# Rows for the gather written once, the accumulator filled by a DRAM copy, and weight splits moved between engines

## The chip, the cores and the metric

One core of a Trainium2 chip runs the kernel. The metric is the device time of one execution in microseconds (us); the median of several executions counts. The engines are named as in the profile: PE is TensorE (PEld its weight loads), DVE is VectorE, ACT is ScalarE, POOL is GpSimd, SP is SyncE, which here only issues DMAs.

## The reference, cut to what matters

One encoder layer over L = 528 tokens (16 meta tokens and 512 real ones) of width 1024. Two attention branches give `oa` and `ob`; these are merged, projected and added to the residual `h`. Then each of 16 experts picks the 66 tokens with the highest affinity to it.

```python
merged = sigmoid(ga) * (oa @ w_branch_a) + sigmoid(gb) * (ob @ w_branch_b)
h = h + merged @ w_out
u = rms_norm(h, g_ffn)
aff = softmax(u @ w_router)                       # (528, 16)
top_aff, top_idx = top_k(aff.T, 66)               # per expert
xs = u[top_idx]                                   # (16, 66, 1024)
y = (silu(xs @ w_gate) * (xs @ w_up)) @ w_down * top_aff
h = h.at[top_idx].add(y)                          # rows are added up
return rms_norm(h, g_final)[16:]
```

## The kernel before

Everything is float32. A product is made of three passes of TensorE: each operand is split into a high half (rounded to the matmul's type) and a low half (the rest), and high x high, low x high and high x low are added up. The helper `hi_lo` (line 440) does one split: ScalarE casts the high half, then VectorE, or the engine that is handed in, subtracts it from the source.

**Order of work.** Instructions for ScalarE, VectorE and GpSimd are not issued where they stand: `Pace` (line 126) keeps them in a list, prices them, follows a model of the engines' clocks and issues the one that can start, a lower `prio` number first. TensorE's instructions and DMAs go out where they stand in the program. Every engine then runs its own list in order, and so do the DMA queues of SP and GpSimd.

**Projections.** `project` (line 500) computes one block of 128 output features for all 528 tokens, in two parts of 256 and 272 columns, 24 matmuls each. It is a generator that yields after 6, 12, 18 and 24 matmuls of a part, so that its caller can put other products between. The weights of the block after it are split inside it by `split_weights` (line 484), in two halves of 128x512; `spare_engine` (line 444) hands the subtraction to GpSimd unless its clock in the model is far ahead. Blocks go by numbers `j`; `jof["yb", 0]` is the first block of w_branch_b, and the eight blocks of w_out come after the eight of w_branch_b.

**w_out and the router** (lines 1298 to 1356). For block d of w_out the evacuation adds the residual into `h2T` (the new `h`, features on the partitions), splits it into `hh` and `hl`, and squares it for the norm. Router products of block d (`sums`) and the column sums of the squares (`ones_sum`) are put into `routed` and taken out of it while block d+1 runs, one after each of the first yields. In the last block (d = 7), ahead of it, the first of the experts' weight pieces is split (`split_piece(0)`, line 1347), the subtraction on GpSimd.

**Routing** (lines 1357 to 1477). `put_rows(t)` turns 88 tokens of `h2T` into rows (8 transposes, two copies by ScalarE) and stores them twice over SP's queue: 1024 wide into `acc`, the accumulator in DRAM to which experts add, and, in `send_rows` (line 1388), 1028 wide into `urow`, from which experts gather, once GpSimd has put the token's norm factor behind its row. There are six groups of 88; the last is stored in two parts, since the meta tokens stand last in the work and first in DRAM. Meanwhile VectorE computes the softmax `lg` and nine rounds of top-k (lines 1448 to 1456), and from both halves of the tokens the list `idxu`. Between, pieces 1 and 2 of the first expert's weights are split (lines 1433 and 1434), on GpSimd again.

**Experts** (lines 1481 to 1701). `gather(e)` fetches 66 rows of `urow` by an indirect DMA of GpSimd; `spread_x(e)` turns them back and applies `g_ffn`; the norm factor comes in as a scale after the first products. The weights are 48 matrices of 2 MB (`mats`, in order of use: gate 0, up 0, gate 1, down 0, up 1, gate 2, down 1, up 2, ...), each used in four pieces of 128x1024, which are split a few pieces ahead. Matrices 1 and on go through a ring of eight buffers (line 1210): matrix n uses buffer (n - 1) mod 8. `load_mat` (line 1221) loads matrices up to 7 over SP's queue and later ones over GpSimd's, matrix 7 in two halves, the second (`load_rest`) over GpSimd's queue behind the first gathers. `scatter(e)` adds the expert's rows to `acc` by an accumulating indirect DMA of GpSimd.

Of the kernel before, what the change touches and what calls it, by code (L numbers as in the profile page):

```python
# [10 lines left out]
F32 = mybir.dt.float32  # L11
F32R = mybir.dt.float32r
# [8 lines left out]
P = 128  # L21
D = 1024
S = 512
M = 16
L = S + M
HL = L // 2
LX = L + 2 * M
DX = D + 4
HALF = [slice(0, 256), slice(256, L)]
NC = D // P  # L30
# [39 lines left out]
def keys(ap):  # L70

    kind = ap.name.split("_")[0]
    step = ap.ap[0][0]
    width = {"kbuf": L, "m1": L, "h2T": L, "xin": D, "pair": L, "obf": L, "hrow": D, "junk": D, "big": D, "first": D, "raw": D,
             "hid": FF // 2, "hhl": 2 * CAP, "xg": 4 * CAP}.get(kind, step)
    rows = {"zp": 32, "kbuf": 64, "qh": 64, "ql": 64, "kbh1": 64, "kbl1": 64}.get(kind, P) if K["kr"] else P
    if width == step and rows == P:
        return {ap.name}
    low, first = divmod(ap.offset, step)
    last = first + sum((n - 1) * s for s, n in ap.ap[1:])  # L80
    high = low + ap.ap[0][1] - 1
    return {f"{ap.name}/{j}/{i}" for i in range(first // width, last // width + 1)
            for j in range(low // rows, high // rows + 1)}
# [209 lines left out]
def block_kernel(ctx: ExitStack, tc: tile.TileContext, x, meta_tokens, g_mix, w_cols,  # L293
# [3 lines left out]
    pace = Pace()  # L297
    Pace.LAT, Pace.AHEAD = K["lat"], K["ahead"]
    nc = Engines(pace, tc.nc)
# [18 lines left out]
    wk = pool(ctx, "wk")  # L318
    psum = pool(ctx, "psum", space=PSUM)
    acc = dram.tile([L, D], F32, name="acc")  # L320
    urow = dram.tile([L, DX], F32, name="urow")
# [78 lines left out]
    def until(*tiles):  # L400

        for _ in range(400):
            if all(pace.when(a) <= pace.now() for a in tiles):
                break
            pace.t["tensor"] = pace.now() + 100.0
            pace.pump()
# [33 lines left out]
    def hi_lo(hi, lo, src, eng=None):  # L440
        nc.scalar.copy(hi, src)
        (eng or nc.vector).tensor_sub(lo, src, hi.bitcast(F32))

    def spare_engine():
        return nc.gpsimd if pace.t.get("gpsimd", 0.0) < pace.now() + K["spare"] else nc.vector
# [25 lines left out]
    loaded, split = {}, {}  # L471
# [12 lines left out]
    def split_weights(j, upto=2):  # L484
        if j >= len(stream):
            return
        load_weights(j)
        if j not in split:
            split[j] = (wk.tile([P, NC, P], F32R, tag="wh", bufs=2, name="wh"),
                        wk.tile([P, NC, P], F32R, tag="wl", bufs=2, name="wl"), [0])  # L490
        wh, wl, done = split[j]
        while done[0] < upto:
            b = slice(4 * done[0], 4 * done[0] + 4)
            with rank(pace, "split"):
                hi_lo(wh[:, b], wl[:, b], loaded[j][:, b], spare_engine())
            done[0] += 1
            if done[0] == 2:
                Task(load_later(j + 3), Need([wl]))
# [42 lines left out]
    jof = {}  # L541
# [17 lines left out]
    xin = [keep.tile([P, 2, D], F32, tag=t, name="xin") for t in ("o_l", "o_h")]  # L559
# [81 lines left out]
    m1 = keep.tile([P, NC, L], F32, tag="m1", name="m1")  # L641
# [329 lines left out]
    kbuf = keep.tile([P, 2, 4, L], F32R, tag="obf", name="kbuf")  # L971
# [107 lines left out]
    obf = keep.tile([P, NH, L], F32, tag="obf", name="obf")  # L1079
# [59 lines left out]
    for h in range(NH):  # L1139
        todo = dict(q=lambda: proj_q(h + 1), k=lambda: proj_k(1), v=lambda: proj_v(1),  # L1140
                    g=lambda: gate_a(h + 1), y=lambda: branch_a(h))
# [15 lines left out]
    pc = pool(ctx, "pc")  # L1157
    mg_h = pc.tile([P, NC, L], F32R, tag="mg_h", name="mg_h")
    mg_l = pc.tile([P, NC, L], F32R, tag="mg_l", name="mg_l")
# [18 lines left out]
    h2T = keep.tile([P, NC, L], F32, tag="obf", name="h2T")  # L1178
# [33 lines left out]
    raws = {}  # L1212
# [3 lines left out]
    def load_rest():  # L1216
        for raw, src in rest:
            nc.gpsimd.dma_start(raw, src)
        rest.clear()

    def load_mat(n, parts=1):
        if n >= len(mats) or n in raws:
            return
        src, kc, f = mats[n]
        src = src.rearrange("(c p) f -> p c f", p=P)
        if n == 0:
            raws[n] = [pc.tile([P, 2, f], F32, tag=("xa", "xb")[i % 2], bufs=2, name="first") for i in range(4)]
            for i, raw in enumerate(raws[n]):
                nc.sync.dma_start(raw, src[:, 2 * i:2 * i + 2])
                raws[n][i] = raw.rearrange("p c f -> p (c f)")  # L1230
            return
        pool_, tag = ring[(n - 1) % len(ring)]
        raw = pool_.tile([P, kc, f], F32, tag=tag, name="raw")
        eng = nc.gpsimd if n > 7 else nc.sync
        cut = kc // parts
        eng.dma_start(raw[:, :cut], src[:, :cut])
        if parts > 1:
            rest.append((raw[:, cut:], src[:, cut:]))
        raw = raw.rearrange("p c f -> p (c f)")
        raws[n] = [raw[:, 1024 * i:1024 * (i + 1)] for i in range(4)]  # L1240

    places = []
    for _ in range(2):
        pair = pc.tile([P, 2, L], F32, tag="ys", bufs=2, name="pair")
# [24 lines left out]
    pieces = {}  # L1269
    whole = {len(mats) - 4: None, len(mats) - 1: None}  # L1270
    nextraw = [9]
    wh, wl, xa, xb = (wk, "wh"), (wk, "wl"), (pc, "xa"), (pc, "xb")
    spots = [(xb, wl), (wh, wl), (xa, xb), (xa, wh)]

    def split_piece(k):
        n, i = divmod(k, 4)
        if n >= len(mats) or k in pieces:
            return
        load_mat(n)
        src = raws[n][i]  # L1280
        if n in whole:
            if i == 0:
                whole[n] = [keep.tile([P, 4, 1024], F32R, tag=tag, name="big") for tag in ("u_h", "u_l")]
            hi, lo = whole[n][0][:, i], whole[n][1][:, i]
        else:
            tags = spots[i if k else 1]
            hi, lo = [pool_.tile([P, 1024], F32R, tag=tag, bufs=2, name=name)
                      for (pool_, tag), name in zip(tags, ("eh", "el"))]
        prio, pace.prio = pace.prio, 2 if n < len(mats) - 2 else K["sp"]
        hi_lo(hi, lo, src, nc.gpsimd if k < 3 or n in whole and i > 1 else None)  # L1290
        pace.prio = prio
        pieces[k] = hi, lo
        if i == 3 and k > LOOK:
            while nextraw[0] <= min(n + len(ring) - (n - 1) // K["skip"], len(mats) - 3):
                load_mat(nextraw[0])
                nextraw[0] += 1
# [46 lines left out]

    load_mat(0)
    for d in range(NC):
        if d == NC - 1:
            split_piece(0)
        g = project(jof["wo", d], mg_h, mg_l, route(d))
        todo = len(routed)
        for n, _ in enumerate(g):  # L1350
            if n < todo:
                routed.pop(0)()
        if d in K["ld"]:
            load_mat(3 + K["ld"].index(d))
# [4 lines left out]
    TQ, NT, HT = 88, 6, 3  # L1359
# [9 lines left out]
    rowq = []  # L1369

    def put_rows(t):
        row = (pc.tile([TQ, DX], F32, tag="ys", bufs=2, name="row") if t == 3 else
               wk.tile([TQ, DX], F32, tag="wraw", bufs=3, name="row"))
        for b in range(2):
            pt = ptr()
            for c in range(4):
                tr(pt[:TQ, c * P:(c + 1) * P], h2T[:, 4 * b + c, t * TQ:(t + 1) * TQ])
            nc.scalar.copy(row[:, 512 * b:512 * b + 512], pt[:TQ, :])
        send(acc, t, row, D)
        rowq.append((t, row))  # L1380

    def send(dst, t, row, w):
        n = TQ if t + 1 < NT else S - t * TQ
        nc.sync.dma_start(dst[M + t * TQ:M + t * TQ + n, :], row[:n, :w])
        if n < TQ:
            nc.sync.dma_start(dst[:M, :], row[n:, :w])

    def send_rows():

        for t, row in rowq:  # L1390
            nc.gpsimd.tensor_copy(row[:, D:], rc[:, t:t + 1].to_broadcast([TQ, DX - D]))
            send(urow, t, row, DX)
        rowq.clear()

    pace.prio = 1
    put_rows(0)
# [15 lines left out]
    rs, rc, sm = cc[:, 1, :NT], cc[:, 1, NT:], cc[:, 3, :NT]  # L1412
# [13 lines left out]
    nc.vector.reciprocal(sm, sm)  # L1426
    nc.vector.tensor_mul(lg, lg, wide(sm))
    pace.prio = 1
    put_rows(1)
    put_rows(2)  # L1430
    pace.prio = 0
    until(lg)
    split_piece(1)
    split_piece(2)
    pf = pz()
    for i in range(HT):
        tr(pf[:2 * NE, i * TQ:(i + 1) * TQ], lg[:, 2 * i:2 * i + 2, :].rearrange("p h e -> p (h e)"))
    pace.prio = 1
    send_rows()
    for t in range(3, NT):  # L1440
        put_rows(t)
        send_rows()
    load_mat(7, parts=2)

    pace.prio = 0
    rounds = (CAP + 7) // 8
# [28 lines left out]
    nc.vector.tensor_tensor(affc, lists[:, 0, 0], vb_, op=OP.max)  # L1475

    until(idxu)
    pace.prio = 1
    xsplit = {}

    def gather(e):
        if e >= NE:
            return
        xs = wk.tile([CAP, DX], F32, tag="wraw", bufs=3, name="xs")
        nc.gpsimd.indirect_dma_start(out=xs, out_offset=None, in_=urow,
                                     in_offset=bass.IndirectOffsetOnAxis(ap=idxu[:, e:e + 1], axis=0))
        xsplit[e] = xs
# [56 lines left out]

    gather(0)
    gather(1)
    gather(2)
    load_rest()
    load_mat(8)
    pace.prio = 0  # L1550
    until(xsplit[0])
# [228 lines left out]
```

## Time and profile before

| | before |
|---|---|
| median of 3 runs | 1058.24 us (1058.0 to 1058.52) |
| the profiled execution itself | 1060.26 us |
| its span, first to last instruction | 1058.5 us |
| TensorE / VectorE / ScalarE / GpSimd busy | 91% / 69% / 60% / 35% |
| mean granted TensorE clock, share of full speed | 0.974 |
| DMA: moved in all | 186.43 MB |

The profile is of one execution. "Busy" counts instructions in execution; matmuls are pipelined, so a busy TensorE need not be at its peak. A row in square brackets names the idle time in front of an instruction and what ended it. All instructions bear line 199 (L199), because one helper issues them all; they are told apart by their tiles, output first ("hl<-h2T,hh"). The blocks of w_out run from about 659 to 719 us, routing to 752 us, the experts to the end.

### The profile page before, as it was taken

The numbers are of one execution on the slowest core, as the hardware profiler recorded it, in microseconds if no ns is written. First come the engines' busy times: TensorE is split into PE (matmuls) and PEld (weight loads), VectorE is DVE, ScalarE is ACT, GpSimd is POOL, SyncE is SP. The second block draws the span as 40 slices with busy tenths as digits, with TensorE's granted clock in tenths as the row PEclk, the third lists the DMA queues.
The fourth block names the chain that finished last, engine by engine and source line by source line (L and its number), as shares of the span: only waits on it lengthen the run. The fifth ranks groups of instructions, "written<-read, shape, count | busy, mean of one in ns | idle before, by whom it ended". The sixth has DMA issues, their size and how long they took to land.

```text
span 1058.5 us, 18096 instructions
## 1 busy us (share of the span) xinstructions
PE 964.3 (91%) x6835; PEld 831.8 (79%) x6835; DVE 726.4 (69%) x1354; ACT 630.2 (60%) x1297; POOL 368.4 (35%) x395
## 2 busy tenths in 40 slices
PE   5799999999999999999999999985599999999984
PEld 4799989999889899999999999873356666666562
DVE  6357777767775666665653345566499999999885
ACT  5366656665655455555554533334388888888773
POOL 3233232333443343443333334432224342424153
PEclk9999999999999999999999999997699999999997
DMA  7544434443222221221212555816799999999964
GB/s 249 168 128 102 134 116 128 132 113 102 68 57 68 71 67 55 71 63 59 71 44 81 160 167 197 326 51 226 244 326 375 337 381 326 377 350 355 343 175 184
DMA packets 59405, 186.43 MB, mean 176 GB/s; under 512 B 6298, under 2 KB 6439, under 8 KB 59318
## 3 DMA queue, kind: packets, MB, share of 16 engines
q1 hardware_dynamic: 32950, 87.96, 26.8%
q0 software_dynamic: 25760, 95.16, 26.2%
q10 hardware_dynamic: 608, 2.16, 0.6%
q8 instruction: 54, 0.88, 0.3%
q14 instruction: 33, 0.27, 0.1%
HBM read 162.07 MB, written 10.76 MB: 163 GB/s over the span
## 4 chain that ended last, share of the span: by engine, by line
PE 61%; DVE 14%; ACT 8%; issue 6%; DMA 5%; POOL 5%; SPq 2%; POOLq 0%; ACTq 0%; DVEq 0%
PE pz L199 36%; PE psc L199 19%; PE ptr L199 5%; DVE sn L199 3%; POOL cols L199 3%; ACT sn L199 2%; SPq L199 2%; DVE cols L199 1%; DVE pb L199 1%; DVE hl L199 1%; DMA raw<-in_w_down_dram 1%; DVE wtl L199 1%; DVE zb L199 1%; DVE ls L199 1%; DMA zp<-zb 1%
## 5 line engine op out<-in xcount | busy, mean ns | idle before, releaser
L199 POOL TENSOR_TENSOR wl<-wraw,wh 128x512 fp32r<-128x512 f32 x137 | 185.3, 1362 | 406.0 <-ACT wh L199 399.6
L199 PE MATMUL pz<-u_h,wh 128*128 128x256 f32 (+1 forms) x832 | 246.2, 296 | 5.7 <-DVE kbuf L199 1.7
L199 PE MATMUL pz<-u_h,wl 128*128 128x256 f32 (+1 forms) x832 | 238.1, 286 | 0.6 <-DVE wl L199 0.6
L199 PE MATMUL pz<-u_l,wh 128*128 128x256 f32 (+1 forms) x832 | 238.0, 286 | 0.5 <-DVE u_l L199 0.5
L199 DVE TENSOR_TENSOR el<-raw,eh 128x1024 fp32r<-128x1024 f32 x180 | 213.9, 1228 | 6.2 <-ACT eh L199 4.9
L199 ACT CAST eh<-raw 128x1024 fp32r<-128x1024 f32 x180 | 182.0, 1049 | 23.8 <-PE pz L199 15.1
L199 PEld LDWEIGHTS pz<-u_h,wh 128*128 128x128 f32 x832 | 158.1, 190 | 9.0 <-DVE kbuf L199 2.3
L199 PEld LDWEIGHTS pz<-u_l,wh 128*128 128x128 f32 x832 | 158.3, 190 | 0.6 <-DVE u_l L199 0.6
L199 PEld LDWEIGHTS pz<-u_h,wl 128*128 128x128 f32 x832 | 157.9, 190 | 0.8 <-DVE wl L199 0.8
L199 PE MATMUL psc<-eh,xh 128*66 128x512 f32 (+1 forms) x272 | 105.1, 386 | 2.7 <-ACT hid L199 2.2
L199 ACT CAST wh<-wraw 128x512 fp32r<-128x512 f32 x152 | 90.9, 616 | 24.0 <-PE pz L199 11.4
L199 PE MATMUL psc<-el,xh 128*66 128x512 f32 (+1 forms) x272 | 104.0, 382 | 0.9 <-DVE el L199 0.9
L199 PE MATMUL psc<-eh,xl 128*66 128x512 f32 (+1 forms) x272 | 104.0, 382 | 0.0
L199 DVE TENSOR_TENSOR wtl<-ptr,wth 128x512 fp32r<-128x512 f32 (+1 forms) x72 | 46.0, 638 | 59.1 <-ACT wth L199 58.8
L199 PE MATMUL pz<-eh,hhl 128*66 128x512 f32 x224 | 70.6, 396 | 0.7 <-DVE hhl L199 0.6
L199 POOL DMA_INDIRECT acc<-ys,idxu x15 | 28.7, 1911 | 119.9 <-ACT ys L199 117.6
L199 ACT ACTIVATE sn<-sn,nm 128x528 f32<-128x528 f32 x64 | 47.1, 736 | 35.2 <-DVE nm L199 34.8
L199 ACT CAST wth<-ptr 128x512 fp32r<-128x512 f32 (+1 forms) x72 | 39.1, 543 | 40.3 <-PE ptr L199 39.9
L199 PEld LDWEIGHTS psc<-eh,xh 128*66 128x66 f32 x272 | 37.5, 138 | 25.4 <-ACT hid L199 3.2
L199 PEld LDWEIGHTS psc<-el,xh 128*66 128x66 f32 x272 | 37.3, 137 | 24.4 <-DVE el L199 1.4
L199 PEld LDWEIGHTS psc<-eh,xl 128*66 128x66 f32 x272 | 37.4, 138 | 21.8 <-issue 0.6
L199 DVE CUSTOM_DVE_ANT_0 sn<-psc,m 128x528 f32<-128x528 f32 x64 | 44.1, 695 | 6.7 <-PE psc L199 6.7
(314 smaller groups left out, 2341.2 us busy)
## 6 DMA issues: line engine op xcount, KB each, us to landing
wraw<-in_w_in_dram SPq DMA_DIRECT2D x76, 512.0 KB
raw<-in_w_gate_dram POOLq DMA_DIRECT2D x13, 2048.0 KB, 14.6
raw<-in_w_down_dram POOLq DMA_DIRECT2D x13, 2048.0 KB, 16.1
raw<-in_w_up_dram POOLq DMA_DIRECT2D x13, 2048.0 KB, 14.9
m<-in_c_bias_dram SPq DMA_DIRECT2D x8, 1056.0 KB
kbuf<-kbuf SPq DMA_DIRECT2D x32, 132.0 KB
raw<-in_w_up_dram SPq DMA_DIRECT2D x2, 2048.0 KB
raw<-in_w_gate_dram SPq DMA_DIRECT2D x2, 2048.0 KB
```

Of the source, the lines that this page charges most:

```text
L199: op.fn(*op.args, **op.kw)
```

## The change

Five things change. (1) From w_branch_b's first block on VectorE subtracts in every weight split. (2) The products in `routed` are taken out after the 12th matmul of the first part and the 6th and 18th of the second, where before it was after the 6th, 12th and 18th of the first part. (3) A row is stored once, 1024 wide, into `urow`; rows 2 to 5 have a tile of their own in a buffer that w_out leaves free (`mg_l`); the norm factors are widened by one GpSimd instruction and stored behind all rows (`send_factors`). (4) `acc` is filled by one DMA from `urow` on GpSimd's queue behind gathers 0 and 1, and matrix 7 is loaded whole on that queue just ahead of it. (5) Pieces 0 to 2 are no longer split on GpSimd in w_out and in routing: the high halves of pieces 0 and 1 are cast behind the rows (`start_piece`), and their low halves and piece 2 follow on VectorE behind the list.

```diff
@@ split_weights @@
-                hi_lo(wh[:, b], wl[:, b], loaded[j][:, b], spare_engine())
+                hi_lo(wh[:, b], wl[:, b], loaded[j][:, b], nc.vector if j >= jof["yb", 0] else spare_engine())
@@ load_mat @@
-        eng = nc.gpsimd if n > 7 else nc.sync
+        eng = nc.gpsimd if n > 6 else nc.sync
@@ new, ahead of split_piece @@
+    def start_piece(k):
+        hi, lo = [wk.tile([P, 1024], F32R, tag=tag, bufs=2, name=name) for tag, name in (("wh", "eh"), ("wl", "el"))]
+        prio, pace.prio = pace.prio, 2
+        nc.scalar.copy(hi, raws[0][k])
+        pace.prio = prio
+        return hi, lo
@@ split_piece @@
-        hi_lo(hi, lo, src, nc.gpsimd if k < 3 or n in whole and i > 1 else None)
+        hi_lo(hi, lo, src, nc.gpsimd if n in whole and i > 1 else None)
@@ blocks of w_out @@
-        if d == NC - 1:
-            split_piece(0)
         g = project(jof["wo", d], mg_h, mg_l, route(d))
         todo = len(routed)
         for n, _ in enumerate(g):
-            if n < todo:
+            if n in (1, 4, 6)[:todo]:
                 routed.pop(0)()
@@ routing @@
     def put_rows(t):
-        row = (pc.tile([TQ, DX], F32, tag="ys", bufs=2, name="row") if t == 3 else
-               wk.tile([TQ, DX], F32, tag="wraw", bufs=3, name="row"))
+        if t == 2:
+            rowq.append(pc.tile([TQ, 4, D], F32, tag="mg_l", name="rowp"))
+        row = (rowq[0][:, t - 2] if t > 1 else pc.tile([TQ, D], F32, tag="ys", bufs=2, name="row") if t else
+               wk.tile([TQ, D], F32, tag="wraw", bufs=3, name="row"))
...
-        send(acc, t, row, D)
-        rowq.append((t, row))
+        send(urow, t, row)
...
-    def send_rows():
-        for t, row in rowq:
-            nc.gpsimd.tensor_copy(row[:, D:], rc[:, t:t + 1].to_broadcast([TQ, DX - D]))
-            send(urow, t, row, DX)
-        rowq.clear()
+    def send_factors():
+        rc4 = pc.tile([TQ, NT, DX - D], F32, name="rc4")
+        nc.gpsimd.tensor_copy(rc4, rc.unsqueeze(2).to_broadcast([TQ, NT, DX - D]))
+        n = NT - 1
+        nc.sync.dma_start(urow[M:M + n * TQ, D:].rearrange("(t p) w -> p t w", p=TQ), rc4[:, :n])
+        send(urow, n, rc4[:, n], slice(D, DX))
...
-    put_rows(1)
-    put_rows(2)
+    for t in range(1, 4):
+        put_rows(t)
     pace.prio = 0
     until(lg)
-    split_piece(1)
-    split_piece(2)
...
-    send_rows()
-    for t in range(3, NT):
+    for t in range(4, NT):
         put_rows(t)
-        send_rows()
-    load_mat(7, parts=2)
+    send_factors()
+    firsts = [start_piece(k) for k in range(2)]
...
     until(idxu)
+    for k, (hi, lo) in enumerate(firsts):
+        nc.vector.tensor_sub(lo, raws[0][k], hi.bitcast(F32))
+        pieces[k] = hi, lo
+    split_piece(2)
...
     gather(0)
     gather(1)
+    load_mat(7)
+    nc.gpsimd.dma_start(acc, urow[:, :D])
     gather(2)
-    load_rest()
     load_mat(8)
```

## Rows read from the trace of the kernel before

**Rows 1.** The page, first part: busy us (share of the span) xinstructions.
```profile
PE 964.3 (91%) x6835; PEld 831.8 (79%) x6835; DVE 726.4 (69%) x1354; ACT 630.2 (60%) x1297; POOL 368.4 (35%) x395
```
**Rows 2.** Waits of PE, 540 to 720 us: us in total, times, longest.
```profile
PE psc L199 <- DVE hl L199: 6.4, 8, 2.0
```
**Rows 3.** Timeline around one w_out block's start: start us, us, instruction [idle before].
```profile
690.95 0.43 DVE L199 TENSOR_TENSOR hl<-h2T,hh 128x256 fp32r<-128x256 f32 x1 [0.47 <-ACT hh L199]
...
693.69 2.74 POOL L199 TENSOR_TENSOR wl<-wraw,wh 128x512 fp32r<-128x512 f32 x2 [4.27 <-ACT wh L199]
...
694.01 1.27 DVE L199 TENSOR_TENSOR hl<-h2T,hh 128x272 fp32r<-128x272 f32 x1 [0.48 <-ACT hh L199]
...
694.40 0.28 PE L199 MATMUL pz<-mg_h,wl 128*128 128x256 f32 x1
...
694.52 0.29 PE L199 MATMUL psc<-hh,wr 128*32 128x272 f32 x1
...
695.34 0.30 PE L199 MATMUL psc<-hl,wr 128*16 128x272 f32 x1 [0.53 <-DVE hl L199]
```
**Rows 4.** Timeline of PE in the last w_out block.
```profile
708.55 0.29 PE L199 MATMUL psc<-hh,wr 128*32 128x272 f32 x1
710.87 0.30 PE L199 MATMUL psc<-hl,wr 128*16 128x272 f32 x1 [2.03 <-DVE hl L199]
...
712.63 0.28 PE L199 MATMUL psc<-qql,ones 128*2 128x256 f32 x1 [0.47 <-DVE qql L199]
```
**Rows 5.** Instructions on tile wl, 600 to 720 us: ns min/median/max, first and last start.
```profile
L199 DVE TENSOR_TENSOR wl<-wraw,wh x2: 692/996/1301, 599.6 to 612.7; 128x512 fp32r<-128x512 f32 x2
```
**Rows 6.** Stretches: length; PE, PEld, DVE, ACT, POOL busy; PEclk, DMA share, GB/s.
```profile
613.00:663.00 50.00, 50.00 (x411) 49.67 (x410) 26.30 (x51) 16.74 (x36) 22.50 (x17) 1.00 0.58 191
663.00:702.00 39.00, 36.17 (x291) 34.25 (x289) 22.70 (x32) 14.72 (x35) 15.67 (x13) 1.00 0.65 241
746.00:786.00 40.00, 33.20 (x152) 19.96 (x153) 28.34 (x34) 26.61 (x32) 12.36 (x15) 0.85 0.86 284
787.00:805.00 18.00, 18.00 (x88) 10.96 (x87) 16.85 (x19) 15.31 (x19) 6.30 (x6) 1.00 1.01 361
```
**Rows 7.** Timeline of ACT, then of DVE, in the routing.
```profile
723.33 1.06 ACT L199 COPY row<-ptr 88x512 f32<-88x512 f32 x2 [0.30 <-PE ptr L199]
724.84 0.28 ACT L199 ACTIVATE lg<-lg 88x96 f32<-88x96 f32 x1 [0.45 <-DVE lg L199]
...
732.75 1.06 ACT L199 COPY row<-ptr 88x512 f32<-88x512 f32 x2 [4.65 <-DMA urow<-row]
...
739.49 0.17 DVE L199 TENSOR_TENSOR idxu<-take,ptr 66x16 uint32<-66x16 f32 x1
```
**Rows 8.** Timeline of SP's DMA issues in the routing.
```profile
721.14 3.56 SPq L199 DMA_DIRECT2D acc<-row  x3
```
**Rows 9.** The chain that ended last, merged: start us, us, what.
```profile
740.68 3.85 DMA urow<-row
...
745.51 6.00 DMA xs<-urow,idxu
...
776.44 0.51 PE ptr L199 x8
...
988.42 9.73 PE psc L199 x42
```
**Rows 10.** Timeline of DVE and POOL around two later gathers.
```profile
825.29 3.48 DVE L199 TENSOR_TENSOR el<-raw,eh 128x1024 fp32r<-128x1024 f32 x3
...
825.51 1.88 POOL L199 DMA_INDIRECT xs<-urow,idxu  x1 [0.21 <-POOL rsx L199]
...
872.39 1.02 POOL L199 DMA_INDIRECT xs<-urow,idxu  x1 [0.21 <-POOL rsx L199]
```
**Rows 11.** Weight loads issued at 763.44 and 958.16 us: KB, us to landing.
```profile
raw<-in_w_down_dram POOLq DMA_DIRECT2D x1, 2048.0 KB, 8.0
...
raw<-in_w_gate_dram POOLq DMA_DIRECT2D x1, 2048.0 KB, 24.3
```

More of the change, by code (lines that the diff above doesn't have):

```diff
@@ L73, in keys @@
     step = ap.ap[0][0]
-    width = {"kbuf": L, "m1": L, "h2T": L, "xin": D, "pair": L, "obf": L, "hrow": D, "junk": D, "big": D, "first": D, "raw": D,
+    width = {"kbuf": L, "rowp": D, "m1": L, "h2T": L, "xin": D, "pair": L, "obf": L, "hrow": D, "junk": D, "big": D, "first": D, "raw": D,
              "hid": FF // 2, "hhl": 2 * CAP, "xg": 4 * CAP}.get(kind, step)
@@ L1285, in split_piece @@
         else:
-            tags = spots[i if k else 1]
+            tags = spots[i]
             hi, lo = [pool_.tile([P, 1024], F32R, tag=tag, bufs=2, name=name)
@@ L1378, in put_rows, with send @@
             nc.scalar.copy(row[:, 512 * b:512 * b + 512], pt[:TQ, :])
-        send(acc, t, row, D)
-        rowq.append((t, row))
-    def send(dst, t, row, w):
+        send(urow, t, row)
+    def send(dst, t, row, cs=slice(0, D)):
         n = TQ if t + 1 < NT else S - t * TQ
-        nc.sync.dma_start(dst[M + t * TQ:M + t * TQ + n, :], row[:n, :w])
+        nc.sync.dma_start(dst[M + t * TQ:M + t * TQ + n, cs], row[:n])
         if n < TQ:
-            nc.sync.dma_start(dst[:M, :], row[n:, :w])
-    def send_rows():
-        for t, row in rowq:
-            nc.gpsimd.tensor_copy(row[:, D:], rc[:, t:t + 1].to_broadcast([TQ, DX - D]))
-            send(urow, t, row, DX)
-        rowq.clear()
+            nc.sync.dma_start(dst[:M, cs], row[n:])
+    def send_factors():
[4 more added lines that the diff above has]
+        send(urow, n, rc4[:, n], slice(D, DX))
     pace.prio = 1
```

## The prediction, written before the change was run

> **What bounds the kernel now.** I read the page first: TensorE is busy for nine tenths of the span [rows 1], so a change pays only where TensorE waits, in the rest. Then the waits of TensorE, the timeline around the longest, the chain of waits through the routing, and last the DMA issues of the expert phase.
>
> In the projection by w_out TensorE waits eight times for hl, VectorE's low half of the residual stream, 6.4 us in all [rows 2]. One block shows the cause [rows 3]: VectorE's subtraction for the first half of the columns takes 0.43 us; that for the second takes 1.27 us, and it runs while GpSimd subtracts the next weights (2.74 us for two). TensorE starts the router product that needs it at 695.34, where its step before (694.40 to 694.52) would put it at 694.64.
>
> Routing is one chain: softmax, top-k, list of rows (idxu), gather, first expert. The list is there at 739.49 + 0.17 = 739.66 [rows 7], but the first gather starts at 745.51, behind the last store into urow, which lands at 744.53 [rows 9]. Those stores are late because a row tile is free only when its second store has landed (ScalarE idles 4.65 us for that [rows 7]) and because SP issues fourteen stores, 1.2 us each in [rows 8].
>
> In the expert loop TensorE does not wait (18.00 us busy of 18), while the DMA engines are full, at 361 GB/s [rows 6]: there the change can only lose.
>
> **The change, part by part.** The sum is made against the profiled execution, 1060.26 us: a span of 1058.5 and 1.76 around it. The median of the runs is 2.02 us lower, 1058.24; I take the gain off that, as nothing ties the difference to a place.
>
> *Weight splits of w_branch_b and w_out from GpSimd to VectorE; router products later.* Each of six blocks (d = 1 to 6) loses 695.34 - 694.64 = 0.70 us: 4.20. In the last block GpSimd also splits the first weight piece, and the losses are 710.87 - 708.55 - 0.12 = 2.20 and, for the column sums, 0.47 [rows 4]. Both halves of the edit take them away: GpSimd no longer subtracts beside VectorE, and the second product, now 12 matmuls into the next block, comes 30 in, some 2 us later. Gain 6.87. The wait behind the last block, with no block to hide it, stays. VectorE pays 32 subtractions of 0.69 us (the shorter of its two, the other ran beside GpSimd) [rows 5]: 1.4 us per block, in two stretches where it was busy 26.3 of 50 and 22.7 of 39 us [rows 6]; the products that need them start a block later. If that cover is gone, a block waits up to 0.69: 16 of them, 11 us. Bounds: 4 and 7.5 gained with the cover, 4 lost without it.
>
> The Trainium skill, "SBUF — State Buffer", section "Who interferes with whom", has a VectorE instruction with two SBUF inputs and a GpSimd one that reads SBUF exclude each other for a whole instruction. The trace agrees: 0.43 against 1.27 us.
>
> *The chain to the gather.* Gone are the second stores with their landing, and two weight pieces' splits in front of row 3's copies. All rows are then turned one behind the other. Row 2 is copied by 723.33 + 1.06; three more at 1.06 and 0.3 us for the gap, and 1 us for Exp and the transposes of the softmax's output between, make 729.5 on the old clock of events. SP needs to 731 to send the last (two stores), and 3.85 of landing [rows 9] make 735. The factors, in stores of 16-byte pieces, have no like in the trace: sent at once, 1.5 us of issue and the same landing, they are there at 736.4; held until the rows have landed, at 740.3. I take the first, since SP sent stores to different rows of one tensor without waiting [rows 8]; the second costs 0.6. So the gather waits for the list. With the 0.98 us between release and start that the chain has (744.53 to 745.51 [rows 9]) it starts at 740.64, a gain of 4.87.
>
> Three things go off. Row 3's first copy (half of 1.06) may stand ahead of the softmax's Exp [rows 7]: 0 to 0.5, taken 0.25. VectorE now computes the low halves of pieces 0 to 2 right behind the list: three took 3.48 us [rows 10], hidden under the gather's 6.00 [rows 9]; but a gather issued while VectorE subtracts took 1.88 us against 1.02 with VectorE idle [rows 10]: 0 to 0.9, taken 0.86. The transfer may be shorter than 6.00 without a weight load beside it: 0 to 1 gained, taken 0. Net 4.87 - 1.11 = 3.76, bounds 2.8 and 6.
>
> By the section just named a subtraction leaves GpSimd's write side free, so what it holds at a gather could only be the read of the list; if that read came first, nothing would be held and the sum would be 0.86 better. Rows 10 show one held.
>
> *The copy within DRAM, and matrix 7 behind the gathers.* GpSimd's queue gets, behind gather 1, the whole of matrix 7 (before, SP loaded half of it ahead of the gathers), the copy of 2.16 MB, then gather 2 and matrix 8, and every later load stands behind these. SP loses seven stores into acc, which lay under the top-k but for their place between the urow stores. No row has a transfer from DRAM to DRAM. Lower bound: a load of nearly its size, with no other load in front, landed in 8.0 us [rows 11]. Upper: its bytes are read and written, so twice that, 16.0. I take 11, nearer the load, since reads and writes can overlap.
>
> Added work is 2.9 us (1.05 MB at 361 GB/s) and 11; the engines were idle 14% of 746 to 786, 5.6 us [rows 6]. So later loads land up to 8.3 us later, and stay so, since DMA is full from 787 on. The tightest load I found is the gate of expert 14: issued at 958.16, landed at 982.5 [rows 11]. Its first product follows 24 of the run of 42 that starts at 988.42 and takes 9.73 [rows 9]: 994.0, less 2.3 us of splitting: 9.2 us of slack. It covers 8.3; up to 11.9 us of copy nothing waits. Gather 2, also behind the copy, is wanted 776.44 - 745.51 = 30.9 us after the start of gather 0 [rows 9], with 6.0 (gather), 5.8 (2.1 MB) and 11 us of transfers before its own: some 8 us of room. Taken: 0; at 16 us the loss is 4.1.
>
> The Trainium skill, "DMA: Bandwidth & Descriptors", section "Specifications", gives some 358 GB/s of HBM per core; as an estimate the copy, 4.32 MB in both directions, would take 12.1 us by it and the sum would be 0.2 us worse. No row here tests it.
>
> Sum: 6.87 + 3.76 - 0 = 10.63, so 1049.6 for the execution that was profiled and 1058.24 - 10.63 = **1047.6 us** for the median.
>
> **The rivals.**
> *Weights late.* The copy takes 12 to 20 us. For it: late loads already land after 24.3 us. Against: DMA had idle time just where the copy goes. 16 us give 1047.6 + 4.1 = 1051.7. Chance 0.17.
> *The gather still waits for urow,* by factors that are held or small pieces that land slowly: 0.6 to 3 us, 1048.2 to 1050.6. For it: the last store bounds the gather today. Against: 3 us of room. Chance 0.11.
> *VectorE becomes the bound* of the two projections, so that the first part loses 4 where it should gain 6.87: 1058.5, no change. For it: one of its two weight splits took about 1.3 us. Against: half its time is free, and a split has a block's lead. Chance 0.04.
> *Slower: the copy blocks the weight stream.* It decides from 11.9 + 10.6 = 22.5 us of copy (96 GB/s): then what every expert's weights come late is more than the gain. At 30 us: 1047.6 + 18.1 = 1065.7. For it: nothing shows how fast DRAM to DRAM goes, and one queue carries it and the weights. Against: 528 rows of 4 KB spread over the engines like the weights. Chance 0.05.
> *More than forecast:* gather not held and shorter, 1044 to 1045.7. Chance 0.08.
>
> **How the numbers follow.** The forecast has 0.55, its own range 1045.7 to 1049.8. To take in a copy of 16 us and a late gather I give 1044.5 to 1052.0; outside lie the two cases at 1058 and beyond, the worse part of the late weights, and a little below. A measurement of this kernel tells 0.2%, 2.1 us, from no change. Faster: forecast, late weights, late gather and more, 0.91. Same: VectorE, 0.04. Slower: 0.05.
>
> **What would show it.** After: no wait of TensorE for hl in the w_out blocks, that behind the last one ending near 711.5; VectorE's hl at 0.43 and its weight splits at 0.69 us. The list near 733.0; the first gather within a microsecond of it, released by VectorE and not by a store; the first expert product near 742.7. The landing time of the copy, and no wait of TensorE for el before the last two experts. I am wrong if a store releases the gather, if weights make TensorE wait, or if the span is not near 1047.9.

## The result, and the profile after

The changed kernel takes 1047.8 us (median of 4 runs, 1047.58 to 1050.28), the kernel before 1058.38 us beside it (1058.0 to 1060.21): a ratio of 0.989, 95% interval 0.9874 to 0.9905. The forecast was 1047.6. A second run of the changed kernel, on another chip, gave 1048.31 us against 1059.26, a ratio of 0.9888 (0.9866 to 0.9911).

The profiled execution took 1047.58 us, its span 1045.8, which is 12.7 less than before. Five starts cut both spans into stretches that can be laid side by side: w_out's first projection matmul, its last, the list, the first gather, the first expert product.

| stretch | before, us | after, us | gain | predicted |
|---|---|---|---|---|
| ahead of w_out | 658.95 | 657.63 | 1.32 | 0 |
| w_out, first to last projection matmul | 57.63 | 50.45 | 7.18 | 6.87 |
| to the list | 22.91 | 23.07 | -0.16 | -0.25 |
| list to first gather | 6.02 | 1.21 | 4.81 | 4.87 |
| first gather to first expert product | 7.77 | 7.46 | 0.31 | -0.86 |
| first expert product to the end | 305.22 | 305.98 | -0.76 | 0 |

The first row can't be told from the spread: over all the profiles of the changed kernel and its variants w_out starts anywhere from 657.19 to 659.56 us. It is 1.32 of the 2.1 us by which the two profiled executions differ more than the two medians do.

**w_out.** TensorE's waits of 540 to 720 us, answering [rows 2]: one for hl is left of eight, the one behind the last block (us in total, times, longest).

```profile
PE psc L199 <- DVE hl L199: 1.2, 1, 1.2
PE pz L199 <- DVE lg L199: 1.2, 1, 1.2
```

The timeline of a block, answering [rows 3]: VectorE's weight split takes 0.69 us and hl 0.44, for 1.27 before; hl is there at 696.85, the product that reads it comes at 698.99 and waits for nothing. The last two lines are TensorE's first and last projection matmul in w_out.

```profile
695.80 0.69 DVE L199 TENSOR_TENSOR wl<-wraw,wh 128x512 fp32r<-128x512 f32 x1
696.41 0.44 DVE L199 TENSOR_TENSOR hl<-h2T,hh 128x272 fp32r<-128x272 f32 x1
...
698.87 0.29 PE L199 MATMUL psc<-hh,wr 128*32 128x272 f32 x1
698.99 0.29 PE L199 MATMUL psc<-hl,wr 128*16 128x272 f32 x1
...
657.63 0.29 PE L199 MATMUL pz<-mg_h,wh 128*128 128x256 f32 x1
...
708.08 0.29 PE L199 MATMUL pz<-mg_h,wl 128*128 128x272 f32 x1
```

**Routing.** The timeline of ScalarE, SP, VectorE and GpSimd, answering [rows 7 and 8]. Row 3's first copy (716.08) stands ahead of the softmax's Exp (716.56), as foreseen. The factors (rc) leave at once behind the rows, at 721.96. The list is there at 731.32; the gather starts 1.04 us later, no store in between ("issue" says that the profile shows nothing that ended its wait), and takes 2.15 us on GpSimd beside VectorE's three subtractions, where the second gather takes 0.95.

```profile
716.08 0.58 ACT L199 COPY rowp<-ptr 88x512 f32<-88x512 f32 x1 [0.24 <-PE ptr L199]
716.56 0.28 ACT L199 ACTIVATE lg<-lg 88x96 f32<-88x96 f32 x1
...
715.86 6.00 SPq L199 DMA_DIRECT2D urow<-rowp  x5
721.96 2.48 SPq L199 DMA_DIRECT2D urow<-rc  x3
...
731.15 0.17 DVE L199 TENSOR_TENSOR idxu<-take,ptr 66x16 uint32<-66x16 f32 x1
731.24 3.67 DVE L199 TENSOR_TENSOR el<-first,eh 128x1024 fp32r<-128x1024 f32 x3
...
732.36 2.15 POOL L199 DMA_INDIRECT xs<-urow,idxu  x1 [15.98 <-issue]
734.81 0.95 POOL L199 DMA_INDIRECT xs<-urow,idxu  x1 [0.31 <-issue]
```

**The copy and the expert phase.** The DMA issues of 735.6 to 737.0 us (KB, us to landing): the copy, issued at 736.72, lands at 751.47; matrix 7, issued at 735.77 ahead of it on the queue, at 745.83. So behind matrix 7 the copy takes 5.6 us.

```profile
acc<-urow POOLq DMA_DIRECT2D x1, 2112.0 KB, 14.8
raw<-in_w_up_dram POOLq DMA_DIRECT2D x1, 2048.0 KB, 10.1
```

Two stretches, with the columns of [rows 6]: just ahead of the gather the DMA engines move nothing; from 740 us on they are full.

```profile
728.00:732.00 4.00, 0.89 (x4) 0.55 (x4) 2.97 (x12) 0.00 (x0) 0.00 (x0) 0.50 0.00 0
...
740.00:750.00 10.00, 10.00 (x39) 5.79 (x40) 6.86 (x8) 5.69 (x7) 1.29 (x2) 0.73 1.01 377
```

The chain that ended last (followed back from the last instruction, at each step to what released it), answering [rows 9]: the first transfer lands 5.69 us after its issue starts, although 1.1 of that is the longer issue. The run of products at 958.26 is not followed by the next at once; TensorE gets a late el at 970.86 and again at 979.92. Those two have no like at that place before, where such lines come only one expert later.

```profile
732.36 5.69 DMA xs<-urow,idxu
...
739.82 8.36 PE psc L199 x24
...
958.26 9.67 PE psc L199 x42
...
968.49 1.06 ACT eh L199
...
969.58 1.24 DVE el L199
...
970.86 2.50 PE pz L199 x10
...
978.64 1.24 DVE el L199
...
979.92 6.67 PE psc L199 x28
```

### The profile page after: what moved, and what is told of

Read it like the earlier page. It is cut to its first block, busy times and chain, and to the rows that moved or that the text cites. A ratio compares the mean times of both kernels' runs of the same rounds, so it can differ in the third digit from the quotient of the medians.

```text
span 1045.8 us, 18076 instructions
## 1 busy us (share of the span) xinstructions
PE 961.1 (92%) x6835; PEld 830.2 (79%) x6835; DVE 728.9 (70%) x1388; ACT 630.1 (60%) x1297; POOL 324.0 (31%) x357
## 3 DMA queue, kind: packets, MB, share of 16 engines
q10 hardware_dynamic: 608, 2.16, 0.6%
## 4 chain that ended last, share of the span: by engine, by line
PE 63%; DVE 14%; ACT 7%; issue 5%; DMA 5%; POOL 4%; SPq 1%; POOLq 0%; ACTq 0%; DVEq 0%
PE pz L199 39%; PE psc L199 20%; PE ptr L199 5%; DVE sn L199 3%; POOL cols L199 3%; ACT sn L199 2%; DVE cols L199 1%; DVE pb L199 1%; SPq L199 1%; DVE ls L199 1%; DVE wtl L199 1%; DVE zb L199 1%; DMA hrow<-acc 1%; DMA xin<-in_x_dram 1%; POOL big L199 1%
## 5 line engine op out<-in xcount | busy, mean ns | idle before, releaser
L199 POOL TENSOR_TENSOR wl<-wraw,wh 128x512 fp32r<-128x512 f32 x106 | 142.0, 1346 | 345.1 <-ACT wh L199 337.7
```

Source lines behind the costliest of these rows:

```text
L199: op.fn(*op.args, **op.kw)
```

## The experiments

Medians from different chips tell no effect of 1 us, so each run is read by its stretches, with its median beside them. The theory: the first edit ends the stall in w_out, the gather waits for the list alone, and the copy is bytes that hide. The rivals: another part of the change did it, or the copy costs something that the sum hides.

**1 and 2. One half of the first edit undone at a time.**

```diff
 e1_gpsimd_splits
-                hi_lo(wh[:, b], wl[:, b], loaded[j][:, b], nc.vector if j >= jof["yb", 0] else spare_engine())
+                hi_lo(wh[:, b], wl[:, b], loaded[j][:, b], spare_engine())
 e2_early_products
-            if n in (1, 4, 6)[:todo]:
+            if n < todo:
```

> The changed kernel with one half of the first edit undone: the weight splits of w_branch_b and w_out subtract on GpSimd again, the router products stay at their later places. Theory A (either half suffices): VectorE's subtraction for hl takes about 1.27 us again beside GpSimd's, but the product that needs it comes 30 matmuls into the next block, so TensorE does not wait in blocks 1 to 6; after the last block, which has no block behind it, hl is up to 0.8 us later. 1047.8 to 1048.7 us. Theory B (the contention on hl was the whole cause): six waits of about 0.7 us come back, 1051.5 to 1053 us.

> The changed kernel with the other half undone: the router products are taken out after the 6th, 12th and 18th matmul of the first part again, VectorE keeps the weight splits. Theory A (either half suffices): hl takes 0.43 us with GpSimd idle and is there when the product comes, 12 matmuls into the block; no wait, or the 0.69 us of a VectorE weight split in front of hl in some blocks: 1047.8 to 1049. Theory B (the place of the products was the whole cause): six to seven waits of about 0.7 us come back, 1051.5 to 1053 us.

Splits undone: 1048.72 us (1046.59 to 1049.6), and w_out takes 50.45 us, the same to the hundredth. Its VectorE timeline has hl at 1.27 us again, but no product is near enough to wait:

```profile
697.93 1.27 DVE L199 TENSOR_TENSOR hl<-h2T,hh 128x272 fp32r<-128x272 f32 x1 [0.49 <-ACT hh L199]
```

Products undone: 1049.08 us (1047.26 to 1050.36), w_out 51.58 us, 1.13 more. No wait for hl in the blocks either; TensorE's timeline has one wait, for the column sums, and the rest is 0.1 us a block. Theory A holds for both. With the products moved, moving the splits gains nothing in w_out; with the splits moved, the place of the products is worth 1.13 us.

```profile
705.32 0.28 PE L199 MATMUL psc<-qql,ones 128*2 128x256 f32 x1 [0.46 <-DVE qql L199]
```

**3. Both halves undone** (both lines above).

> The changed kernel with both halves of the first edit undone: weight splits on GpSimd and router products early, everything else as changed. With one half undone at a time, TensorE's w_out blocks took 50.45 us (splits undone) and 51.58 us (products undone) from first to last projection matmul, 50.45 us in the changed kernel and 57.63 before. Theory A (each half alone removes the stall, only both undone bring it back): six waits for hl of about 0.5 us, 54.7 us or more for the blocks (the first piece's split, which made the last block worse, stays off GpSimd), 1052 us. Theory B (the stall had another cause, such as that first piece's split or the stores): under 52 us, 1048 to 1049.

1051.04 us (1050.78 to 1051.66), w_out 55.30 us: 4.85 more than the changed kernel, 2.33 less than before. The waits of TensorE, 655 to 725 us, have the six of 0.53 us back (the longest wait, 1.2, is the one behind the last block):

```profile
PE psc L199 <- DVE hl L199: 4.4, 7, 1.2
```

So theory A, and more exactly: with the fifth part in place, the first edit is worth 4.85 us. The other 2.33 lie in the last block alone (9.67 us before, 7.34 here; the others take the same in both), and there the fifth part takes away the first weight piece's split. In the kernel before, VectorE's hl took 2.38 us beside that split, by the timeline of GpSimd and VectorE:

```profile
708.16 2.36 POOL L199 TENSOR_TENSOR el<-first,eh 128x1024 fp32r<-128x1024 f32 x1 [4.71 <-ACT eh L199]
708.43 2.38 DVE L199 TENSOR_TENSOR hl<-h2T,hh 128x272 fp32r<-128x272 f32 x1 [0.89 <-ACT hh L199]
```

**4. No copy within DRAM: the rows stored a second time, behind the factors.**

```diff
+    for t, row in enumerate(kept):
+        send(acc, t, row)
...
-    nc.gpsimd.dma_start(acc, urow[:, :D])
```

> The changed kernel without the copy within DRAM: the accumulator is filled by a second store of each row from SBUF over SP's queue behind the factors, as many stores as before the change but behind all that the gather needs. Theory A (the gain in the routing comes from the gather waiting for the list and not for a store; how the accumulator is filled is free): the first gather still starts within 1.1 us of the list, TensorE's start on the experts is unchanged, and the time is 1046.5 to 1048, the lower end if the order in experts 11 to 13 comes back. Theory B (the second stores themselves hold the gather, because they share SP's queue and the DMA engines with the factors): the gather starts 1 to 4 us later and the time is 1049 to 1052.

1047.66 us (1047.42 to 1047.76). The gather starts 1.21 us after the list's start, as in the changed kernel, and the first expert product comes 31.87 us after w_out's last matmul (31.74 there). Theory A: what counted is what stands in front of the gather; the copy as such gains nothing over stores that are out of the way. No run puts the second stores back in front of the gather, so that they held it before is read from the rows. Nor are the later loads earlier without the copy: the weights of expert 14's gate land 246.6 us after the list's start, 245.2 in the changed kernel.

**5. VectorE and the first gather: the first pieces' low halves on GpSimd during the top-k.**

```diff
     def start_piece(k):
...
-        nc.scalar.copy(hi, raws[0][k])
+        hi_lo(hi, lo, raws[0][k], nc.gpsimd)
...
-    firsts = [start_piece(k) for k in range(2)]
+    for k in range(2):
+        pieces[k] = start_piece(k)
+    split_piece(2, nc.gpsimd)
...
-    for k, (hi, lo) in enumerate(firsts):
-        nc.vector.tensor_sub(lo, raws[0][k], hi.bitcast(F32))
-        pieces[k] = hi, lo
-    split_piece(2)
```

> The changed kernel, with the low halves of the first three weight pieces computed by GpSimd during the top-k in place of VectorE behind the list. Theory A (VectorE's subtractions held the first gather): the gather, 2.15 us on GpSimd in the changed kernel, takes 0.95 to 1.05 us as the second did there, TensorE starts the experts about 1.1 us earlier, 1046.7 us. Theory B (the first gather is long for another reason, such as being the first): it stays at 2.1 us and the time at 1047.8. Slower, by up to 2 us, if GpSimd's subtractions hold VectorE's top-k: then the list is late by the same amount.

1045.99 us (1045.61 to 1048.03). The gather starts 0.32 us after the list's end and takes 1.05; from the list's start to the first expert product it is 6.79 us, 8.67 in the changed kernel. Theory A, and larger than I expected: 1.88 us, of which 1.10 is the time that the gather's issue takes and 0.72 its start. The list itself comes no later.

```profile
731.96 0.17 DVE L199 TENSOR_TENSOR idxu<-take,ptr 66x16 uint32<-66x16 f32 x1
...
732.45 1.05 POOL L199 DMA_INDIRECT xs<-urow,idxu  x1 [2.56 <-DVE idxu L199]
```

**6. The late start: GpSimd idle too long, or VectorE?**

```diff
     until(lists)
+    nudge = pc.tile([CAP, 1], F32, name="nudge")
+    nc.gpsimd.tensor_copy(nudge, lists[:, 0, 0, :1])
```

> The changed kernel with one tiny GpSimd instruction, a copy of 66 numbers, that depends on a step 1.1 us before the list. In the changed kernel GpSimd had nothing for 16 us and its first gather starts 1.04 us after the list; with GpSimd busy until 2.6 us before (the run with the pieces on GpSimd) it starts 0.32 us after. Theory A (an engine that has been idle long takes longer to start): the gather starts 0.3 to 0.4 us after the list, 0.7 us earlier. Theory B (VectorE's subtractions, which start with the end of the list, hold the start of the gather as they hold its run): it still starts about 1.04 us after. No more than 0.7 us either way, so the rows tell it and the time does not.

1047.99 us (1047.74 to 1048.91). With GpSimd at work until 2.07 us before, nothing changes: the list is there at 731.80 and the gather starts at 732.83, 1.03 us later. An idle engine is not the reason; what is left of the difference from run 5 is VectorE's subtractions.

```profile
730.58 0.18 POOL L199 COPY nudge<-lists 66x1 f32<-66x1 f32 x1 [13.75 <-DVE lists L199]
732.83 2.15 POOL L199 DMA_INDIRECT xs<-urow,idxu  x1 [2.07 <-issue]
```

The gather's long time has a condition, though. In the eight runs where the gather starts 1.11 or 1.12 us after the first subtraction it takes 2.15 to 2.17 us. In runs 1 and 3 it starts 1.03 and 1.04 us after it, beside the same subtractions, and takes 1.11 and 1.10. Runs 1 and 3 are the two that keep the weight splits on GpSimd; whether that tenth of a microsecond decides or something else of that edit, no run shows. Nor are subtractions beside a gather enough to hold it: in the kernel before, the one at 813.67 us stands wholly beside two that follow each other from 813.68 on, and takes 1.02. The timeline of GpSimd and VectorE in run 1:

```profile
732.96 3.70 DVE L199 TENSOR_TENSOR el<-first,eh 128x1024 fp32r<-128x1024 f32 x3
...
733.99 1.11 POOL L199 DMA_INDIRECT xs<-urow,idxu  x1 [15.91 <-DVE idxu L199]
```

**7. The late el in the experts: the copy priced at nothing in the planner.**

```diff
-            return (CAP * D if "indirect" in self.op else n * self.outs[0].shape[0]) * 4 / 360.0
+            return (CAP * D if "indirect" in self.op else 0 if self.outs[0].name.startswith("acc") else n * self.outs[0].shape[0]) * 4 / 360.0
```

> The changed kernel, with the copy within DRAM priced at nothing in the planner. The DMAs, TensorE's and GpSimd's orders stay the same; what changes is the order in which ScalarE and VectorE work in experts 11 to 13. In the changed kernel TensorE loses 1.26 us in expert 13's period (18.66 us for 17.4). Theory A (the planner issued another order because it believes the DMA late): that period is back at 17.4 us and the time falls by about 1.3 us, to 1046.5. Theory B (weights really land too late): the period stays at 18.66 us and the time at 1047.8.

1048.17 us (1047.26 to 1048.97) on another chip, where before took 1059.42: the medians don't tell 1.3 us. The chain does, in its first and last run of products here. From 959.14 it runs on without a late el to the next products, and reaches the end of those at 976.49 + 9.69 = 986.18, 27.04 us after 959.14; the changed kernel takes 979.92 + 6.67 - 958.26 = 28.33. The copy goes at the same place in both, so the 1.29 us were lost to the order in which the planner (`Pace`), which believed the DMA late, issued ScalarE's and VectorE's work. No weight was late. Theory A.

```profile
959.14 9.67 PE psc L199 x42
...
976.49 9.69 PE psc L199 x42
```

**8. How much slack there was: two more copies** (on run 7's kernel).

```diff
     nc.gpsimd.dma_start(acc, urow[:, :D])
+    nc.gpsimd.dma_start(acc2, urow[:, :D])
+    nc.gpsimd.dma_start(acc3, urow[:, :D])
```

> The kernel with the unpriced copy, and two more copies of the same rows behind the first on GpSimd's queue, into two tensors in DRAM that nothing reads: 4.3 MB more of copying, all later loads behind it. A test of the slack that the prediction put at 9.2 us at the gate of expert 14. The one copy took about 5.7 us by the landing times of the changed kernel, so two more push the loads by about 11.3 us. Theory A (slack of 9.2, of which matrix 7's 2.9 us and the first copy's 5.7, less the idle 5.6, use some 3): 6.2 us are left, TensorE waits for el late in the experts and the time is about 5 us above the kernel with one unpriced copy, 1051 to 1052. Theory B (the DMA stream has far more slack): no difference, 1046.5. Theory C (no slack left, every late byte costs): 11 us more, 1057 to 1058.

1058.93 us (10 runs, 1054.81 to 1062.41), 10.8 above run 7. By the number that is theory C, but the rows show two places. First gather 2, which stands behind the copies: in run 7 it landed 17.3 us after 738.66, at 755.9, and was wanted at 764.3; here it lands at 768.7. TensorE's timeline, and two stretches (columns of [rows 6]):

```profile
768.83 1.11 PE L199 MATMUL ptr<-ident,xs 66*128 66x66 f32 x8 [4.84 <-DMA xs<-urow,idxu]
```

```profile
760.00:770.00 10.00, 4.54 (x23) 2.74 (x22) 5.12 (x7) 3.67 (x4) 1.49 (x3) 0.83 1.01 313
770.00:780.00 10.00, 10.00 (x37) 5.64 (x36) 7.04 (x9) 7.34 (x10) 3.04 (x3) 0.83 1.03 344
```

The 4.84 us of idle TensorE cost 7.2 by the next run of products (first expert product to it: 34.36 us for 27.16), since the granted clock fell after the idle time, to 0.83 over these 20 us (a mean of its two levels, 1.2 and 2.4 GHz) for 1.00 in run 7. The other 4.8 us go at the end, where the chain stands on a weight load:

```profile
942.35 22.39 DMA raw<-in_w_up_dram
...
964.83 1.06 ACT eh L199
```

How much room the loads had is read at the gate of expert 14, which the prediction took for the tightest: its issue in the changed kernel (948.93 us), in run 7 (948.68) and here (961.81), with KB and us to landing.

```profile
raw<-in_w_gate_dram POOLq DMA_DIRECT2D x1, 2048.0 KB, 27.4
...
raw<-in_w_gate_dram POOLq DMA_DIRECT2D x1, 2048.0 KB, 26.4
...
raw<-in_w_gate_dram POOLq DMA_DIRECT2D x1, 2048.0 KB, 27.9
```

Its first product starts at 982.28, 981.87 and 991.89. Less the 2.3 us of splitting, that leaves 3.7, 4.5 and -0.2 us. Against the list the load comes 15.3 us later than in run 7, and TensorE comes to it 10.6 us later against the first expert product. So theory A's 6 us of slack are not there: run 7 had 4.5, and the eight profiles with one copy at this place have anywhere from 1.2 to 5.5. And the room of gather 2, 8.4 us by run 7's rows, I had left out of the expectation though the prediction gives it.

The copies themselves (KB, us to landing), issued at 737.04, 737.74 and 738.40, land at 752.8, 759.8 and 767.1: 7.0 us for the second and 7.3 for the third.

```profile
acc<-urow POOLq DMA_DIRECT2D x1, 2112.0 KB, 15.7
...
acc<-urow POOLq DMA_DIRECT2D x1, 2112.0 KB, 22.1
...
acc<-urow POOLq DMA_DIRECT2D x1, 2112.0 KB, 28.7
```

**9. The copy early, on SP's queue behind the factors; and 10. that with run 5.**

```diff
     send_factors()
+    nc.sync.dma_start(acc, urow[:, :D])
...
-    nc.gpsimd.dma_start(acc, urow[:, :D])
```

> The changed kernel with the copy within DRAM issued on SP's queue right behind the factors, in a stretch (728 to 732 us) where the DMA engines moved nothing, and no longer on GpSimd's queue behind the gathers; the order in experts 11 to 13 is that of the kernel before. Theory A (the copy is only bytes that can go where DMA is idle): expert 13's period is back at 17.4 us, later loads land about 5 us earlier, 1046 to 1046.6 us. Theory B (the copy, ahead of the first gather, slows that gather's transfer): the first landing takes up to 5.7 us longer than 5.69 us, and the time is 1048 to 1053.

> The copy issued early and the first three pieces' low halves on GpSimd together. If both theories A hold, the gains add: the gather starts as soon as the list is there and takes about 1 us, expert 13's period is 17.4 us, 1045.0 to 1045.8 us. If GpSimd's subtractions or the copy hold the chain to the gather, 1047 to 1050.

Run 9: 1046.77 us (1043.97 to 1047.35); the DMA engines now work where they stood idle, and the first gather lands 5.55 us after its issue starts, 5.69 in the changed kernel. From 958.41 us to the end of the next run of products it is 27.05, as in run 7. Two stretches, and SP's queue (packets, MB, share of the engines) in 728 to 736.6 us:

```profile
728.00:732.00 4.00, 0.73 (x4) 0.53 (x4) 3.20 (x13) 0.00 (x0) 0.00 (x0) 0.50 0.85 274
732.00:736.00 4.00, 0.16 (x2) 0.02 (x1) 3.64 (x8) 1.04 (x1) 2.03 (x1) 0.50 0.84 256
...
q1 hardware_dynamic: 544, 2.16, 79.6%
```

That is the whole copy: its packets run from 728.6 to 736.5 us, and the gather's first starts behind them, at 736.8. So this run does not show what a copy in flight would do to the gather's transfer.

Run 10: 1044.3 us (1042.17 to 1045.16), ratio to before 0.9835 (0.9809 to 0.9861). Theory A of both: the gather starts 0.32 us after the list and takes 1.08, and the gate of expert 14 has 8.9 us to spare. For a comparison on one chip, the changed kernel and run 10's were timed again side by side:

> The changed kernel as it is, for a comparison on one chip with the best of the experiments: 1047.8 us.

> The kernel with the copy early and the first pieces on GpSimd, again, beside the changed kernel: by its rows the first expert product comes 1.9 us sooner after the list and the experts take 1.7 us less, so some 3.5 us below the changed kernel on the same chip.

1048.31 us (1047.95 to 1048.62) and 1045.16 us (1044.25 to 1047.88): 3.15 us apart, no run of the one among those of the other. The list to the first product takes 6.86 us for 8.60, and the experts 303.4 for 305.1.

## Why the prediction was right, and where its steps were not

**The stall in w_out: size right (7.18 for 6.87), one cause left out.** That each half of the first edit takes the waits away is shown by runs 1 to 3, and with it why only both undone bring them back: 0.70 us a block, as predicted. But I put the last block's 2.20 us to that edit alone ("both halves of the edit take them away"); run 3 has 2.33 of the 7.18 without it, by the first piece's split leaving the block. Whether the later place of the product would have covered that wait too, no run shows, as none leaves that split in the block. VectorE's cover held: 0.69 us a split, no product late. That rival is out.

**The gather waits for the list: right.** List to gather 4.81 for 4.87, the delay in front 0.16 for 0.25; the factors left at once. The rival that stores still hold it is out, even with the second stores back behind the factors (run 4). One reading was wrong and did no harm, as the factors had 3 us of room: the three stores of [rows 8] take 0.37, 0.29 and 0.28 us, and the rest of their 3.56 is time between them.

**The hold by VectorE: mis-sized, and covered by another term.** Predicted 0.86. Run 5 shows 1.10 for the gather's time and 0.72 for its start. The 0.98 us that I put between release and start came from a row in which a store released the gather; released by VectorE with nothing beside it, the start comes 0.32 us after. The Trainium skill, "SBUF — State Buffer", section "Who interferes with whom", infers that a subtraction of two SBUF inputs leaves what descriptor generation needs free. These runs show a gather held for 1.1 us beside such subtractions, in eight of ten, so the row was the better guide (though its 1.02 us are not quite "with VectorE idle": a product stands beside the last 0.37). Whether it is held at the read of its list, as the prediction has it, or at something else, no run shows. What made the stretch right on balance is the term that I took as 0 of 0 to 1: the transfer. From the end of the gather's instruction to the landing it took 6.00 - 1.06 = 4.94 us before and 5.69 - 2.15 = 3.54 now, 1.40 less. The prediction's condition for a shorter one, no weight load beside it, is met: before, half of matrix 7 was still moving beside the gather's first packets (SP's queue ends at 748.6 us, the gather's packets start at 747.3), and now nothing else moves then. In the runs too, but for a dozen last packets of other transfers at most, nothing does, and it takes 3.2 to 3.7 us. But no run puts a load back beside it, so the cause of the 1.40 stays open.

**The copy: no loss to late weights, right, by luck as far as sizes go.** The copy took 5.6 us (6.8 in run 7, 7.0 and 7.3 behind another copy in run 8) for an assumed 11 and a lower bound of 8. The bound came from a load that was put alone in its row; alone, as in run 9, the copy too takes 9.2 us from its issue (727.33) to the end of its last packet, and behind a load it is faster. The Trainium skill's "DMA: Bandwidth & Descriptors", section "Specifications", made it 12.1 us as an estimate; the runs show half of that to two thirds. Yet the slack of 9.2 us (9.0 by the product's own row) shrank to 3.7 at the same gate. With a copy of 5.6 my sum gave 2.9 + 5.6 - 5.6 = 2.9 us used, the rows 5.4. The term I left out: TensorE starts the experts 13.46 us earlier, but matrix 8 is issued only 11.1 earlier (738.80 for 749.92), so 2.3 us of lead are lost before the copy costs anything. By the same count a copy of the 11 us that I assumed would have come 2 us late. And one profile doesn't fix such a slack: in the eight with the copy at this place it is 1.2 to 5.5 us.

**What no step had: 1.29 us lost to an order.** "No wait of TensorE for el before the last two experts" failed, one expert early. The transfer was free on the chip and not in the planner, whose price of it moved work of ScalarE and VectorE 220 us later (run 7). The rest of the experts' 0.76 us is two things for which the change has no step: the first run of products, partly at half clock, took 8.36 us for 7.74 (7.36 in the second profile of the changed kernel, where the experts take 305.1 in all), and the tail behind the last run shown took 59.2 us for 60.35 (59.3 in the second profile).

So the sum of 10.63 met the medians' 10.6 in part by luck, with wrong sizes against each other: by the rows 1.2 us more in the gather's stretch, 0.3 in w_out, 0.1 ahead of the list, 0.8 less in the experts, which makes 11.4; the 0.8 to the medians' difference is within the spread of the executions. The span, given as 1047.9, was 1045.8, and 1046.8 in the second profile.

## What to carry to other kernels

Put on the path only what the next step reads, and look for who waits at each issue: here a row's second store cost nothing that the time shows once it stood behind the gather. A transfer that "hides" still has a price in a planner and takes its place on a queue; put it where the DMA engines are idle. When a compute step is put right beside an indirect DMA's issue, price the hold, or give that step to another engine some microseconds earlier.

## What the runs showed that I had not expected

A copy of 2112 KB within DRAM, read and written, took 5.6 us behind the load ahead of it (6.8 in run 7), and 7.0 to 7.9 with no load beside it (landing to landing for run 8's second and third, first packet to last in run 9). A load of its size takes 6.0 us at the 361 GB/s of [rows 6] (2.16 MB). So reading and writing in DRAM cost at most a third more than reading, and not twice as much.

A gather's issue on GpSimd takes 0.95 to 4.46 us, and all those above 1.7 stand beside subtractions of VectorE that follow each other; runs 5 and 10 alone test that the subtractions are the cause, at the first gather. The longest stands beside a product with a scalar and three subtractions without a gap; runs 1, 6 and 7 have it at the same place with the same 4.46. The timeline of VectorE and GpSimd in the changed kernel:

```profile
929.79 0.75 DVE L199 SCALAR_TENSOR_TENSOR hid<-psc,rsx,hid 66x512 f32<-66x512 f32 x1 [0.90 <-ACT hid L199]
930.46 3.48 DVE L199 TENSOR_TENSOR el<-raw,eh 128x1024 fp32r<-128x1024 f32 x3
...
930.37 4.46 POOL L199 DMA_INDIRECT xs<-urow,idxu  x1 [0.20 <-POOL rsx L199]
```
